# Gelu steps beside the gates, reordered against the head merge

## Chip, cores and metric

One core of a Trainium2 chip runs the whole kernel. The metric is the device time of one execution in microseconds (us); lower is better. Three executions of the kernel before are given.

## The reference, cut to what matters

The program is one decoder block for 1,024 tokens of width 1,024 in float32. Only one place of it concerns the change: the joining of two mixers that run side by side.

```python
y = s5_ssm(u, ...)                                    # (1024 tokens, 768 channels)
z = jax.nn.gelu(y) @ w_glu + b_glu
b_ssm = z[..., :1024] * jax.nn.sigmoid(z[..., 1024:])
wts = jax.nn.softmax(jnp.stack(lses, axis=0), axis=0)  # over the 3 dilated head groups
att = jnp.einsum('gbsh,gbshd->bshd', wts, jnp.stack(outs, axis=0))
b_att = att.reshape(bsz, s, 256) @ w_att_up
mixed = jax.nn.sigmoid(g_ssm) * b_ssm + jax.nn.sigmoid(g_att) * b_att
h = layer_norm(ALPHA * h + (mixed @ w_mix_out + b_mix_out), ln1_g, ln1_b)
```

The gates `g_ssm` and `g_att` are products of the normed input with 2,048 columns of `w_in`. The gelu is the one with the tanh in it.

## The kernel before, in words

Every float32 operand of a product is kept as a high part and a low part, and `mm3` (L99 to L102) multiplies high by high, high by low and low by high. So each tensor that feeds TensorE (PE) has two tiles, and each high/low pair costs one cast on ScalarE (ACT) and one subtraction on VectorE (DVE).

The order of instructions is written by hand: the scheduler is switched to manual, and each engine runs its own instructions in the order in which the program issues them. Side work is woven into the products by generators. `slot()` (L272) first moves the weight stream on (`W.pump`: at most one new load on SP's queue, and one split, an ACT cast `whi` at L136 and a DVE subtraction `wlo` at L137), then runs deferred work, and then lets each generator in `sides` go on to its next `yield`. In the gates a `point()` (L1159) calls `slot()` after every 12 products: once in the middle of a half gate (24 products, `gate_half`) and once at its end. At the end of a half gate, ahead of that second point, the gate's own evacuation is issued: a tanh on ACT (L593), a scale on GpSimd (POOL, L594) and a store to `g_dr` on SP's queue (L595). Splits fall at the point that ends a gate's second half.

`merge_side` (L1043) is the generator that runs beside gates 8 to 15. It does two jobs. For each of 8 token tiles `t` it merges the three head groups: `load` (L1052) brings tile `am` in, `m_main` (L1069) computes softmax weights (three small DVE operations, an exp on ACT at L1076, five small DVE operations), multiplies the heads by them (L1083, DVE) and adds the three groups (L1084 and L1085, POOL); `m_tail` (L1062) transposes the result on PE (L1065) and splits it into `ath` and `atl` (ACT L255, DVE L256). And for each of 12 pieces `i` of the SSM output it computes the gelu: `y_a` loads `yb`; `y_b` squares it on ACT into `yv` (L1099) and does a scale and a product on POOL (L1100, L1101); `y_c` does the tanh on ACT (L1107), a fused add and product on DVE (L1108), the high part `yh` on ACT (L1111) and the low part `yl` on DVE (L1112).

The tile `yv` has one buffer, so the square of a piece can't start until the low part of the piece before has been read from it; pieces 9 to 11 use the buffers of `am` instead:

```python
v = mg_p.tile([128, 4, 128], FT, name="yv", tag="yv", bufs=1)
```

Before the change the order was, per tile: at the first point `m_main(t)` and the load of the next `am`; at the second point `m_tail(t-1)`, then `y_tick(t)`: `y_c` of piece `t-1`, `y_b` of piece `t`, and `y_a` of piece `t+1`. So between `y_b` and `y_c` of one piece stands the next tile's `m_main`. After tile 7 come five more points (`y_tick` for 8 to 12), in which `y_b(i)` goes ahead of `y_c(i-1)`. When gates and merge are through, the gated merge starts (L1179): its first products read `yh` and `yl` of all 12 pieces.

Of the kernel before, what the change touches and what calls it, by code (L numbers as in the profile page):

```python
# [21 lines left out]
NT = SEQ // 128  # L22
# [36 lines left out]
def block_kernel(ctx, tc, I, out, dbg=None):  # L59
# [6 lines left out]
    def open_pool(name, side, **kw):  # L66
        p = tc.tile_pool(name=name, bufs=1, side=side, **kw)
        return p, p.__enter__()
# [27 lines left out]
    def axbank(shape):  # L96
        return ps.tile(list(shape), FT, name="ax", tag="ax", bufs=4)
# [3 lines left out]
        pe.matmul(o, lhsT=lh, rhs=rl, start=False, stop=False)  # L101
        pe.matmul(o, lhsT=ll, rhs=rh, start=False, stop=last)  # L102

# [1 line left out]
    class Stream:  # L105
        def __init__(self):
            self.req = []
# [98 lines left out]
        for i in range(4):  # L206
            W.add(I["wff2"][4 * hc + i], 1024)

# [1 line left out]
    stp = con  # L210

    def ln_rstd(sts, e, extra=None):
# [41 lines left out]
    def split_ps(hi, lo, p):  # L254
        act.copy(hi, p)  # L255
        dve.tensor_sub(lo, p, hi.bitcast(FT))  # L256
# [24 lines left out]
                if next(g, "end") == "end":  # L281
                    sides.remove(g)

# [1 line left out]
    kv_c, kvp = open_pool("kv", "left")  # L285
    mem_c, memp = open_pool("memp", "left")
    st_c, stl = open_pool("start", "right")
# [53 lines left out]
        transpose_in(x, hh, hl, t)  # L341
        act.dma_start(h_dr[t], x)

# [1 line left out]
    T = {}  # L345

    def load_bq(g):
# [331 lines left out]
    for n, (b, part) in enumerate(ustep):  # L679
# [4 lines left out]
        if n in (2, 4):  # L684
            q = 1 + n // 2
# [26 lines left out]
    load_bq(1)  # L712
    par_c, parp = open_pool("par", "right")
    sides.append(params(parp))
# [1 line left out]
    ssm_d = None  # L716

    def start_ssm():
# [164 lines left out]
            ds[b].clear()  # L883
            yield

# [1 line left out]
    att_c, att = open_pool("att", "right")  # L887

    def tok(g, n):
# [147 lines left out]

    sides.insert(0, att_tail())

# [1 line left out]
    state = {"att": att_c, "ssm": ssm_c}  # L1041

    def merge_side():  # L1043
        yf_c, yf = open_pool("yf", "left")
        state["yf"] = yf_c
        ath = yf.tile([128, 2, SEQ], FR, name="ath")
        atl = yf.tile([128, 2, SEQ], FR, name="atl")
        yh = yf.tile([128, 6, SEQ], FR, name="yh")
        yl = yf.tile([128, 6, SEQ], FR, name="yl")
        state.update(ath=ath, atl=atl, yh=yh, yl=yl)  # L1050

        def load(t):  # L1052
            a = mg_p.tile([128, 3, 264], FT, name="am", tag="am", bufs=3)
            sp.dma_start(a, at_dr[:, 128 * t:128 * t + 128, :].rearrange("g p f -> p g f"))
            return a

        mg_c, mg_p = open_pool("mg", "right")
        state["mg"] = mg_c
        nxt = load(0)
        que = deque()  # L1060

        def m_tail(t, a):  # L1062
            p = axbank((128, 2, 128))
            for k in range(2):
                pe.transpose(p[:, k, :], a[:, 0, 128 * k:128 * k + 128], ident)  # L1065
            s = slice(128 * t, 128 * t + 128)
            split_ps(ath[:, :, s], atl[:, :, s], p)

        def m_main(t, a):  # L1069
            w = mg_p.tile([128, 32], FT, name="mw", tag="mw", bufs=2)  # L1070
            M, dd, e, den = w[:, 0:4], w[:, 4:16].rearrange("p (g h) -> p g h", g=3), \
                w[:, 16:28].rearrange("p (g h) -> p g h", g=3), w[:, 28:32]
            dve.tensor_max(M, a[:, 0, 260:264], a[:, 1, 260:264])
            dve.tensor_max(M, M, a[:, 2, 260:264])
            dve.tensor_sub(dd, a[:, :, 260:264], M[:, None, :].to_broadcast([128, 3, 4]))
            act.activation(e, dd, AF.Exp, scale=ATT_SCALE)  # L1076
            dve.tensor_mul(dd, e, a[:, :, 256:260])
            dve.tensor_add(den, dd[:, 0, :], dd[:, 1, :])
            dve.tensor_add(den, den, dd[:, 2, :])
            dve.reciprocal(den, den)  # L1080
            dve.tensor_mul(e, e, den[:, None, :].to_broadcast([128, 3, 4]))
            num = a[:, :, 0:256].rearrange("p g (h d) -> p g h d", h=4)
            dve.tensor_mul(num, num, e.rearrange("p g (h o) -> p g h o", o=1).to_broadcast([128, 3, 4, 64]))  # L1083
            pool.tensor_add(a[:, 0, 0:256], a[:, 0, 0:256], a[:, 1, 0:256])  # L1084
            pool.tensor_add(a[:, 0, 0:256], a[:, 0, 0:256], a[:, 2, 0:256])  # L1085

        def y_a(i):
            b, jh = divmod(i, 2)
            y = mg_p.tile([128, 4, 128], FT, name="yb", tag="yb", bufs=2)
            sp.dma_start(y, y_dr[128 * b:128 * b + 128, 4 * jh:4 * jh + 4, :])  # L1090
            return y

        def y_b(i, y):
            if i <= NT:
                v = mg_p.tile([128, 4, 128], FT, name="yv", tag="yv", bufs=1)
            else:
                v = mg_p.tile([128, 3, 264], FT, name="am", tag="am", bufs=3)
                v = v.rearrange("p g f -> p (g f)")[:, 0:512].rearrange("p (j c) -> p j c", j=4)
            act.activation(v, y, AF.Square)  # L1099
            pool.tensor_scalar(v, v, 0.044715, 1.0, op0=OP.mult, op1=OP.add)  # L1100
            pool.tensor_mul(v, v, y)  # L1101
            return v

        def y_c(i, y, v):
            b, jh = divmod(i, 2)
            js = slice(4 * jh, 4 * jh + 4)
            act.activation(v, v, AF.Tanh, scale=float(np.sqrt(2.0 / np.pi)))  # L1107
            dve.scalar_tensor_tensor(v, v, 1.0, y, op0=OP.add, op1=OP.mult)  # L1108
            vp = v.rearrange("p j c -> p c j")
            yhb, ylb = (q[:, b, :].rearrange("p (c j) -> p c j", j=8)[:, :, js] for q in (yh, yl))  # L1110
            act.activation(yhb, vp, AF.Copy, scale=0.5)  # L1111
            dve.scalar_tensor_tensor(ylb, vp, 0.5, yhb.bitcast(FT), op0=OP.mult, op1=OP.subtract)  # L1112

        ys = {0: y_a(0)}
        vs = {}

        def y_tick(i):
            if i in ys and i > NT:
                vs[i] = y_b(i, ys[i])
            if i - 1 in vs:  # L1120
                y_c(i - 1, ys.pop(i - 1), vs.pop(i - 1))
            if i in ys and i <= NT:
                vs[i] = y_b(i, ys[i])
            if i + 1 < 12:
                ys[i + 1] = y_a(i + 1)

        yield
        for t in range(NT):
            m_main(t, nxt)
            que.append((t, nxt))  # L1130
            if t < NT - 1:
                nxt = load(t + 1)
            yield
            if t:
                m_tail(*que.popleft())
            y_tick(t)
            yield
        for i in range(NT, 13):
            y_tick(i)
            yield  # L1140
            if i == NT:
                m_tail(*que.popleft())

    merged = [False]

    def launch_merge():
        if merged[0] or sides:
            return
        close_pool(state["att"])
        close_pool(state["ssm"])  # L1150
        close_pool(stb_c)
        close_pool(tab_c)
        g = merge_side()
        sides.append(g)
        merged[0] = True
# [16 lines left out]
    close_pool(state["mg"])  # L1172
    ath, atl, yh, yl = (state[k] for k in ("ath", "atl", "yh", "yl"))

# [1 line left out]
    mx_c, mx = open_pool("mx", "right")  # L1176
    xh = actp.tile([128, KB, SEQ], FR, name="acth", tag="acth")
    xl = actp.tile([128, KB, SEQ], FR, name="actl", tag="actl")
# [41 lines left out]
    close_pool(mx_c)  # L1220
    close_pool(state["yf"])

# [1 line left out]
    nat_c, nat = open_pool("nat", "left")  # L1224
    hn = nat.tile([128, NT, D], FT, name="hn")

# [52 lines left out]

    nat_gemm(xh, xl, evac_mix)  # L1280

# [1 line left out]
    ptp_c, ptp = open_pool("ptp", "right")  # L1283
    ph = ptp.tile([128, 4, SEQ], FR, name="ph")
    pl = ptp.tile([128, 4, SEQ], FR, name="pl")
# [44 lines left out]

    nat_gemm(Cat(ph, xh), Cat(pl, xl), evac_xo)

# [1 line left out]
    fh, fl = ph, pl  # L1334
    for t in range(NT):
        defer(t, lambda t=t: dve.scalar_tensor_tensor(hn[:, t, :], hn[:, t, :], ALPHA, bf2, op0=OP.mult, op1=OP.add))
# [157 lines left out]
```

## Time and profile before

| | us |
|---|---|
| three executions | 1945.46, 1943.19, 1945.0 |
| median | 1945.0 |
| span of the profiled execution, first to last instruction | 1943.7 |
| TensorE busy, share of the span | 1885.0 (97%) |
| VectorE busy | 966.7 (50%) |
| ScalarE busy | 563.7 (29%) |
| GpSimd busy | 609.0 (31%) |
| mean granted TensorE clock, 1 being full | 0.990 |

The profile gives the span of the profiled execution but no time of its own for it; the median of the three timed executions is 1.3 us above that span. The head merge and the gelu run from about 700 to 791 us of the span.

### The profile page before, as it was taken

What the parts mean: (1) busy time and instruction counts of PE and PEld (TensorE: products, weight loads), DVE (VectorE), ACT (ScalarE), POOL (GpSimd) and SP (SyncE); (2) the same over time, 40 slices, a digit from 0 to 9 for tenths busy, and PEclk for the clock granted to TensorE, in tenths of its full rate; (3) what the DMA queues carried; (4) which work ended last, traced back from release to release, by engine and by line L of the source; (5) the groups of instructions that cost most, each with busy time, mean ns of one, the idle gap of its engine ahead of it and who ended that gap; (6) DMA issues with size and microseconds to landing.
All of it is one profiled execution on the core that took longest, in us unless ns stands there. A gap on an engine that the chain in (4) does not pass through costs nothing.

```text
span 1943.7 us, 24170 instructions
## 1 busy us (share of the span) xinstructions
PE 1885.0 (97%) x9400; PEld 1619.6 (83%) x9400; DVE 966.7 (50%) x1678; ACT 563.7 (29%) x998; POOL 609.0 (31%) x782
## 2 busy tenths in 40 slices
PE   7899999999999998999999999999999999999996
PEld 7798788889999976788888888788888888888885
DVE  6526846675666666444556445542323223232328
ACT  4324343433332434322124322412121212213121
POOL 3305687474565335322034004401010100101016
PEclk9999999999999999999999999999999999999998
DMA  6545562130120243333511121111111111011102
GB/s 243 184 122 187 183 198 73 34 99 23 55 67 29 75 136 109 118 117 109 185 44 44 44 76 44 44 65 44 55 54 44 44 44 66 32 55 48 62 21 87
DMA packets 82563, 163.26 MB, mean 84 GB/s; under 512 B 19857, under 2 KB 39441, under 8 KB 82449
## 3 DMA queue, kind: packets, MB, share of 16 engines
q1 hardware_dynamic: 75968, 147.30, 22.8%
q10 hardware_dynamic: 5904, 12.85, 1.7%
q0 software_dynamic: 576, 1.57, 0.3%
q8 instruction: 74, 1.21, 0.3%
q14 instruction: 41, 0.33, 0.1%
HBM read 126.99 MB, written 34.70 MB: 83 GB/s over the span
## 4 chain that ended last, share of the span: by engine, by line
PE 86%; DVE 7%; ACT 2%; issue 2%; POOL 2%; DMA 1%; DVEq 0%; SPq 0%; ACTq 0%; POOLq 0%
PE mm L100 26%; PE mm L102 26%; PE mm L101 26%; PE ax L262 1%; DVE wlo L137 1%; PE ax L996 1%; PE ax L969 1%; PE ax L987 1%; PE ax L822 1%; ACT yh L1111 1%; PE ax L845 1%; PE ax L954 1%; PE ax L809 1%; DVE lnst L237 0%; PE ax L846 0%
## 5 line engine op out<-in xcount | busy, mean ns | idle before, releaser
L100 PE MATMUL mm<-acth,whi 128*128 128x512 f32 (+1 forms) x896 | 348.0, 388 | 4.9 <-ACT abst L611 4.6
L102 PE MATMUL mm<-acth,wlo 128*128 128x512 f32 (+1 forms) x896 | 345.5, 386 | 2.5 <-DVE wlo L137 2.5
L101 PE MATMUL mm<-actl,whi 128*128 128x512 f32 (+1 forms) x896 | 345.4, 386 | 0.3 <-DVE actl L256 0.3
L136 ACT CAST whi<-wraw 128x1024 fp32r<-128x1024 f32 (+1 forms) x169 | 168.4, 996 | 419.5 <-PE mm L102 300.9
L137 DVE TENSOR_TENSOR wlo<-wraw,whi 128x1024 fp32r<-128x1024 f32 (+1 forms) x169 | 213.2, 1263 | 146.9 <-ACT whi L136 144.6
L100 PE MATMUL mm<-whi,acth 128*128 128x512 f32 (+1 forms) x704 | 281.7, 400 | 0.0
L102 PE MATMUL mm<-whi,actl 128*128 128x512 f32 (+1 forms) x704 | 270.7, 384 | 0.0
L101 PE MATMUL mm<-wlo,acth 128*128 128x512 f32 (+1 forms) x704 | 270.4, 384 | 0.0
L1350 POOL TENSOR_TENSOR sg<-sg 128x512 f32<-128x512 f32 x64 | 67.8, 1059 | 574.4 <-ACT sg L1349 574.4
L100 PE MATMUL mm<-whi,ph 128*128 128x512 f32 x576 | 224.3, 389 | 0.0
L102 PE MATMUL mm<-whi,pl 128*128 128x512 f32 x576 | 224.1, 389 | 0.0
L101 PE MATMUL mm<-wlo,ph 128*128 128x512 f32 x576 | 224.1, 389 | 0.0
L100 PEld LDWEIGHTS mm<-acth,whi 128*128 128x128 f32 x896 | 171.1, 191 | 38.4 <-ACT abst L611 5.5
L102 PEld LDWEIGHTS mm<-acth,wlo 128*128 128x128 f32 x896 | 170.6, 190 | 36.4 <-DVE wlo L137 3.0
L101 PEld LDWEIGHTS mm<-actl,whi 128*128 128x128 f32 x896 | 171.1, 191 | 32.6 <-DVE actl L256 0.5
L102 PEld LDWEIGHTS mm<-whi,actl 128*128 128x128 f32 x704 | 168.0, 239 | 15.3
L101 PEld LDWEIGHTS mm<-wlo,acth 128*128 128x128 f32 x704 | 168.6, 239 | 14.2
L100 PEld LDWEIGHTS mm<-whi,acth 128*128 128x128 f32 x704 | 167.5, 238 | 15.4
L1352 DVE TENSOR_TENSOR pl<-sg,ph 128x512 fp32r<-128x512 f32 x64 | 44.3, 692 | 261.8 <-ACT ph L1351 261.8
L1368 DVE TENSOR_TENSOR hn<-hn,mm 128x512 f32<-128x512 f32 x128 | 87.0, 685 | 163.7 <-PE mm L102 163.7
L102 PEld LDWEIGHTS mm<-whi,pl 128*128 128x128 f32 x576 | 108.1, 188 | 22.4
L101 PEld LDWEIGHTS mm<-wlo,ph 128*128 128x128 f32 x576 | 108.1, 188 | 22.4
(322 smaller groups left out, 2882.6 us busy)
## 6 DMA issues: line engine op xcount, KB each, us to landing
wraw<-in_wff_dram SPq DMA_DIRECT2D x64, 512.0 KB
wraw<-in_wg_dram SPq DMA_DIRECT2D x16, 512.0 KB
gl<-g_dr SPq DMA_DIRECT2D x32, 256.0 KB
wraw<-in_wqk_dram SPq DMA_DIRECT2D x12, 512.0 KB
wraw<-in_wglu_dram SPq DMA_DIRECT2D x16, 384.0 KB
g_dr<-abst SPq DMA_DIRECT2D x16, 256.0 KB
a_dr<-abst ACTq DMA_DIRECT2D x16, 256.0 KB
b_dr<-abst ACTq DMA_DIRECT2D x16, 256.0 KB
```

The source lines that it names most:

```text
L100: pe.matmul(o, lhsT=lh, rhs=rh, start=first, stop=False)
L101: pe.matmul(o, lhsT=lh, rhs=rl, start=False, stop=False)
L102: pe.matmul(o, lhsT=ll, rhs=rh, start=False, stop=last)
L136: act.copy(h[:, :n], r[:, :n])
L137: dve.tensor_sub(l[:, :n], r[:, :n], h[:, :n].bitcast(FT))
L262: pe.transpose(p[:, k, :], x[:, (4 * b + k) * 128:(4 * b + k + 1) * 128], ident)
L809: pe.matmul(p[:, g, :], lhsT=xe[:, g].rearrange("p j o -> p (j o)"), rhs=d["cm"][:, g, 0:8, :].rearrange("p j o -> p (j o)"), start=True, ...
L822: pe.matmul(p[:, g, :], lhsT=d["bt"][:, g, :], rhs=d["U"][:, g, :], start=True, stop=True)
L845: pe.matmul(p[:, g, :], lhsT=dts[:, g, :], rhs=d["U"][:, g, :], start=True, stop=False)
L1350: pool.tensor_mul(r, r, r)
L1352: dve.tensor_sub(fl[:, i, s], r, fh[:, i, s].bitcast(FT))
L1368: dve.tensor_add(hn[:, t, cs], hn[:, t, cs], p)
```

## The change

The subtraction that makes `yl` leaves `y_c` and becomes a step `y_d` of its own. A new `y_first(i)` does `y_d` of the piece before, then `y_a` of the next piece, then `y_b` of piece `i`. In the loop over tiles `y_first(t)` is issued right behind `m_main(t)` at the first point (ahead of the load of the next `am`), and `y_c(t)` at the second point behind `m_tail(t-1)`. So `y_b` and `y_c` of a piece now stand in one tile, with nothing of `m_main` between them, and `yl` of piece `t-1` stands behind `m_main(t)`. After tile 7, each point does `y_c(i)` and then `y_first(i + 1)`, and the last `yl` has a point to itself, behind that point's weight split. The number of points is as before. Otherwise only comment lines of the source fall away, which moves line numbers.

```diff
@@ -1109,37 +1109,44 @@
             act.activation(yhb, vp, AF.Copy, scale=0.5)
+            lows.append((ylb, vp, yhb))
+
+        def y_d():
+            if not lows:
+                return
+            ylb, vp, yhb = lows.pop()
             dve.scalar_tensor_tensor(ylb, vp, 0.5, yhb.bitcast(FT), op0=OP.mult, op1=OP.subtract)
 
+        lows = []
         ys = {0: y_a(0)}
-        vs = {}
-
-        def y_tick(i):
-            if i in ys and i > NT:
-                vs[i] = y_b(i, ys[i])
-            if i - 1 in vs:
-                y_c(i - 1, ys.pop(i - 1), vs.pop(i - 1))
-            if i in ys and i <= NT:
-                vs[i] = y_b(i, ys[i])
+
+        def y_first(i):
+            y_d()
             if i + 1 < 12:
                 ys[i + 1] = y_a(i + 1)
+            return y_b(i, ys[i])
 
         yield
         for t in range(NT):
             m_main(t, nxt)
             que.append((t, nxt))
+            v = y_first(t)
             if t < NT - 1:
                 nxt = load(t + 1)
             yield
             if t:
                 m_tail(*que.popleft())
-            y_tick(t)
+            y_c(t, ys.pop(t), v)
             yield
-        for i in range(NT, 13):
-            y_tick(i)
+        v = y_first(NT)
+        yield
+        m_tail(*que.popleft())
+        for i in range(NT, 12):
+            y_c(i, ys.pop(i), v)
+            if i < 11:
+                v = y_first(i + 1)
             yield
-            if i == NT:
-                m_tail(*que.popleft())
+        y_d()
```

## Rows read from the trace of the kernel before

**Rows 1.** The page's first part: busy time of each engine, whole span.

```profile
PE 1885.0 (97%) x9400; PEld 1619.6 (83%) x9400; DVE 966.7 (50%) x1678; ACT 563.7 (29%) x998; POOL 609.0 (31%) x782
```

**Rows 2.** Busy time by stretch: window, length, PE, PEld, DVE, ACT, POOL, clock, DMA, GB/s.

```profile
712.82:761.44 48.62, 39.15 (x161) 30.45 (x160) 37.76 (x76) 21.68 (x39) 26.98 (x30) 0.93 0.43 139
...
791.00:830.00 39.00, 39.00 (x172) 32.31 (x173) 16.68 (x23) 10.31 (x18) 10.70 (x11) 1.00 0.42 132
```

**Rows 3.** Waits of PE between 690 and 800 us: total, times, longest.

```profile
PE ax L1065 <- POOL am L1085: 9.9, 6, 2.5
```

**Rows 4.** Timeline of one tile: start, duration, engine, line, operands, [idle before <- releaser].

```profile
742.80 1.30 POOL L1101 TENSOR_TENSOR yv<-yv,yb 128x512 f32<-128x512 f32 x1
742.96 1.15 DVE L1079 TENSOR_TENSOR mw<-mw 128x4 f32<-128x4 f32 x1
...
745.72 0.72 POOL L1084 TENSOR_TENSOR am<-am 128x256 f32<-128x256 f32 x1 [1.63 <-PE mm L102]
745.84 1.15 DVE L1108 SCALAR_TENSOR_TENSOR yv<-yv,yb 128x512 f32<-128x512 f32 x1
...
747.03 1.11 ACT L1111 ACTIVATE yh<-yv 128x512 fp32r<-128x512 f32 x1 [2.27 <-DVE yv L1108]
...
747.64 0.44 PE L1065 MATMUL ax<-cst,am 128*128 128x128 f32 x2 [2.01 <-POOL am L1085]
748.17 1.08 DVE L1112 SCALAR_TENSOR_TENSOR yl<-yv,yh 128x512 fp32r<-128x512 f32 x1 [1.17 <-ACT yh L1111]
```

**Rows 5.** Timeline: the product of the heads (L1083) of tiles 1 and 7.

```profile
711.86 0.96 DVE L1083 TENSOR_TENSOR am<-am,mw 128x768 f32<-128x768 f32 x1
...
760.48 0.96 DVE L1083 TENSOR_TENSOR am<-am,mw 128x768 f32<-128x768 f32 x1
```

**Rows 6.** Timeline 764 to 772: gelu of piece 7, no head merge beside it.

```profile
765.14 0.63 ACT L1099 ACTIVATE yv<-yb 128x512 f32<-128x512 f32 x1 [1.15 <-DVE yl L1112]
765.86 0.62 POOL L1100 TENSOR_SCALAR yv<-yv 128x512 f32<-128x512 f32 x1 [1.83 <-ACT yv L1099]
766.56 1.29 POOL L1101 TENSOR_TENSOR yv<-yv,yb 128x512 f32<-128x512 f32 x1
...
768.55 0.69 DVE L1108 SCALAR_TENSOR_TENSOR yv<-yv,yb 128x512 f32<-128x512 f32 x1 [3.44 <-ACT yv L1107]
769.27 1.14 ACT L1111 ACTIVATE yh<-yv 128x512 fp32r<-128x512 f32 x1 [0.76 <-DVE yv L1108]
770.44 1.09 DVE L1112 SCALAR_TENSOR_TENSOR yl<-yv,yh 128x512 fp32r<-128x512 f32 x1 [1.20 <-ACT yh L1111]
```

**Rows 7.** Timeline: merge of tile 0, no gelu beside it: exp to product of heads.

```profile
704.37 0.21 ACT L1076 ACTIVATE mw<-mw 128x12 f32<-128x12 f32 x1 [5.16 <-DVE mw L1075]
...
705.62 0.96 DVE L1083 TENSOR_TENSOR am<-am,mw 128x768 f32<-128x768 f32 x1
```

**Rows 8.** Timeline: a low part on DVE and a gate's scale on POOL at once.

```profile
782.40 1.08 DVE L1112 SCALAR_TENSOR_TENSOR yl<-am,yh 128x512 fp32r<-128x512 f32 x1 [1.21 <-ACT yh L1111]
783.03 0.88 POOL L594 TENSOR_SCALAR sg<-sg 128x512 f32<-128x512 f32 x1 [0.68 <-ACT sg L593]
```

**Rows 9.** Timeline: a weight split's subtraction on DVE.

```profile
736.98 0.95 DVE L137 TENSOR_TENSOR wlo<-wraw,whi 128x768 fp32r<-128x768 f32 x1
```

**Rows 10.** Timeline: the end of the gelu and the gated merge's first waits.

```profile
788.67 1.09 ACT L1111 ACTIVATE yh<-am 128x512 fp32r<-128x512 f32 x1 [1.12 <-DVE am L1108]
...
789.80 1.07 DVE L1112 SCALAR_TENSOR_TENSOR yl<-am,yh 128x512 fp32r<-128x512 f32 x1 [1.16 <-ACT yh L1111]
790.24 0.82 ACT L136 CAST whi<-wraw 128x768 fp32r<-128x768 f32 x1
...
790.92 0.50 PE L101 MATMUL mm<-yl,whi 128*128 128x512 f32 x1 [0.60 <-DVE yl L1112]
```

**Rows 11.** Timeline of PE: transposes of two neighbouring tiles.

```profile
731.21 0.44 PE L1065 MATMUL ax<-cst,am 128*128 128x128 f32 x2 [1.99 <-POOL am L1085]
...
739.71 0.44 PE L1065 MATMUL ax<-cst,am 128*128 128x128 f32 x2 [0.95 <-POOL am L1085]
```

## The prediction, made before the change was run

> **What bounds the kernel now.** The page's first part says PE: busy 97% of the span, DVE only half of it [rows 1]. That is an average, so the next view is busy time by stretch. While the head merge runs, PE is busy 39.15 of 48.62 us at a mean clock of 0.93; right after it, all of 39.00 us at 1.00 [rows 2]. So in this stage something else sets the pace, and what the stage loses is not made good later: behind it PE is full. PE's waits name the culprit: the merge's transposes (L1065) wait for POOL's sum of the head groups (L1085), 9.9 us in 6 waits [rows 3]. Those sums come at the pace of the loop over tiles on DVE, ACT and POOL: from the product of the heads (L1083) of tile 1 to that of tile 7 are 760.48 - 711.86 = 48.62 us, 8.10 per tile [rows 5], against PE's 5.48 for 24 products (from 739.71 + 0.44 to 747.64 - 2.01) and 0.44 for the transposes, 5.92 in all [rows 4, 11].
>
> The loop now: low part of piece t-1, `m_main(t)` on DVE, L1108 of piece t, its high part on ACT, its low part. DVE stands idle 1.17 for the high part [rows 4]. The rest of the gelu, square to tanh, runs on ACT and POOL beside `m_main`, at a price: a 4-element L1079 takes 1.15 us, ending when POOL's L1101 ends at 744.10, where tile 0 went through the exp and all five small operations in 1.25 (704.37 to 705.62) [rows 7], and L1108 takes 1.15 beside L1084 against 0.69 alone [rows 4, 6]. DVE and POOL keep each other out.
>
> **The change, part by part.** Nothing is computed more or less; instructions move.
>
> *Removed.* Per tile, DVE's wait of 1.17 for the high part, and the two stalls, 1.0 and 0.46: about 2.6 us.
>
> *What the new order waits for.* Square to tanh of piece t loses its cover, because `m_main(t)` now stands ahead of it and the square can't start before the low part of piece t-1, now behind `m_main(t)`, has left the single `yv`. And ACT runs the exp of `m_main(t+1)` behind the high part of piece t, so DVE's wait for ACT doesn't go away: it moves from L1112 to L1077, three small operations further on. All steps lie in one ring: low part, square, L1100, L1101, tanh, L1108, high part, exp, L1083, low part.
>
> *Its length.* Piece 7 of the old kernel ran just this ring without the merge. The square starts at 765.14, 0.03 behind the low part before it; L1108 ends at 769.24, the high part at 770.41, the low part at 771.53: 6.42 us a turn [rows 6]. The merge puts in exp to the end of L1083, 2.21 us in tile 0, where no gelu disturbed it (704.37 to 706.58) [rows 7]; with about 0.1 of overlap at either end, 2.0. POOL's two sums now stand ahead of L1100. They can begin as L1083 ends, but the low part is on DVE by then. Where a low part and a POOL operation meet, POOL's takes 0.88 and ends 0.43 behind the low part (783.91 against 783.48) [rows 8], where such a scale takes 0.62 alone [rows 6]. So I let L1084 end 0.59 behind the low part and L1085 take 0.73, near L1084's 0.72 [rows 4]; L1100 then starts 1.49 behind the low part instead of 0.75, which adds 0.74. If POOL weren't held there, the sums would be over before the square and add nothing: that is the lower end. I take the held case, as rows 8 show this very instruction. Together 6.42 + 2.0 + 0.7 = **9.1 us per tile** against 8.10; lower end 8.4.
>
> *Weight splits* (L137) fall into the second point of every other tile. The 0.95 us [rows 9] used to lie between DVE's steps; now they come when POOL does L1101, and one of the two waits: some 0.6 for the two splits of 768 columns, 0.1 for a small one, 1.3 in all; at the least nothing.
>
> *Start.* Before, no gelu step lay between the L1083 of tiles 0 and 1; now one turn of the ring does. Tile 0 has no low part (1.08 less) but a large split (0.95 or more), so I count a full 9.1. L1083 of tile 7 then ends at 706.58 + 7 x 9.1 + 1.3 = 771.6, against 761.44: 10.2 us late.
>
> *End.* From there the old kernel needed 29.4 us to the last low part (790.87) [rows 10], which PE waits for. New: low part of 6, 1.0; on to L1108 of 7, 4.1 + 0.7; high and low part, 2.3; piece 8 to its L1108, 4.1 and 0.4 for a split; its high part, 1.2. That is 13.8. Pieces 9 to 11 are squared only behind the high part of the piece before (formerly ahead of it): 765.14 to 770.41 is 5.27 [rows 6], with 0.25 for L1100 held by the low part, 5.5 each: 30.3. The last low part has moved past the next point's weight split: the cast ends 1.3 behind the last high part (791.06 against 789.76) [rows 10], then `wlo` 0.95 and the low part 1.08: 33.7, or 4.3 us later than before. POOL's scale for a gate may get between those two on DVE: 0.4 more.
>
> *What costs nothing.* `y_a` passes the load of `am` on SP's queue, an issue of some 0.4 us; both tiles are wanted a full turn later. The gate's tanh (ACT) and scale (POOL) now stand behind the square and L1101, so PSUM banks and the two `sg` buffers come free later; PE's waits list none for them and PE itself waits longer at the transposes. Without that cover the late tanh would cost PE up to the 0.63 of the square per half gate, one of three banks in use, so I count zero.
>
> *Sum.* 10.2 + 4.3 + 0.4 = 14.9 us on the profiled span of 1943.7, whose tail is full PE work and hides none of it. The median of the runs is 1945.0, 1.3 above the span; I add the sum to the median: **1960 us**.
>
> *PE's clock.* Behind a wait of 1.99 the next 24 products took 7.11 us (731.65 to 738.76) instead of 5.48, so part of them ran at 1.2 GHz instead of 2.4, 1.63 us lost [rows 11]. In the merge a turn of 9.1 covers that. The Trainium skill, TensorE: Matmul & The Clock Gate, Part 1, says that the throttled state is the default and that activity releases it. By that rule the longer waits, 9.1 - 5.92 = 3.2, speak against the change: a throttle behind every wait. No run here shows it yet. By the rows, the end is the only bare place: PE has done its gates and the first 15 products some 2.6 us ahead of the last high part, then waits some 3 us more for the low part, and a throttle there adds up to 1.6: 1961.6.
>
> **The rivals.**
> *POOL isn't held by the low part, and splits fall into gaps.* The ring is 8.4: 706.58 + 58.8 = 765.4, 4.0 late; the end shorter by 0.7 + 3 x 0.25 + 0.4, so about 2.5 late: +6.5 to +8, 1952. For it: POOL's starts in the trace are often early. Against it: rows 8.
> *Bare throttle at the end*, +16.5, 1961.6; if slow products filled whole half gates (10.96 + 0.44 per turn, 2.3 more than 9.1), seven turns would add 16 to that, near 1977; rows 11 show recovery within the half, so I give this next to nothing.
> *Faster: PE takes the pace.* If a square didn't have to wait for the low part (were `yv` free in time), `m_main` and high part would overlap with the next square, DVE's own work per tile (2.21 + 1.08 + 0.69 and, by my estimate from the lengths of their like, 1.0 for three small operations and the transposes' low part: 5.0 us) would fit under PE's 5.92, and seven turns from 706.58 would end L1083 of tile 7 at 748.0, 13.4 early, less 4.7 at the end: 1936. The place is the wait of L1099 for L1112, which the trace shows ("<-DVE yl L1112") [rows 6]. It decides where a turn is under (761.44 - 4.7 - 1.3 - 706.58) / 7 = 7.0 us, and the ring of durations alone gives 8.4.
> *No change.* A turn of 6.4 to 7.5 us would give it; nothing in the rows is that short. Also the change could do nothing if the low part were held by ACT in either order, but `yv` then still puts the square later.
>
> **How the numbers follow.** Main case 1960: 0.70. Low case 1952: 0.15. Bare throttle 1961.6 or more: 0.08. Faster: 0.03. No change: 0.04. About 0.2%, 3.9 us, is what a measurement can tell from no change. Faster 0.03, same 0.04, slower 0.93. The range goes from the low case, 1952, to the throttle with all splits at their upper price (two more at 0.6, and 1.5 for the start), 1965.
>
> **What would show it.** Right: L1083 ends some 9 us apart; DVE's L1112 no longer waits for ACT but L1077 does, by 0.5 us or more; L1079 back to 0.16; L1084 stretched beyond 1 us beside L1112; DVE idle ahead of L1108, waiting for the tanh; PE's waits at L1065 near 3 us each; the last low part behind `wlo`. Wrong: L1083 less than 7.5 us apart, squares that start without waiting for L1112, or PE waiting for a bank instead of L1085.

## The result, and the profile of the changed kernel

The changed kernel takes **1962.99 us** (median of 4 runs, 1959.36 to 1963.58), the kernel before 1944.75 on the same chip (4 runs): a ratio of 1.0086, 95% interval 1.0074 to 1.0098. It is slower by 18.2 us; the forecast was 1960.0, with a range from 1952 to 1965. The profiled execution took 1963.19, 1.8 above its span of 1961.4 us; the span before was 1943.7. So 17.7 us have to be found in the trace. Of all executions behind the numbers below one took 8133.02 us (the low part alone late, in the kernel before); it is left out, and its cause is not known.

The page's first part is the average that hides the matter. It answers to [rows 1]:

```profile
PE 1892.8 (97%) x9400; PEld 1624.8 (83%) x9400; DVE 954.4 (49%) x1678; ACT 563.5 (29%) x998; POOL 609.8 (31%) x782
```

PE ran the same 9400 products, for 7.8 us more, and its share is again 97%. DVE did the same 1678 instructions in 12.3 us less: the stalls that the change removes are indeed gone. Added up over the eight tiles, the small operations L1073 to L1081 took 10.7 us less and L1108, over all twelve pieces, 2.4 less, together some 1.6 a tile; a little of it came back in other operations. The time went elsewhere. The waits of PE between 690 and 815 us, as total, times and longest, answer to [rows 3]:

```profile
PE ax L1065 <- POOL am L1085: 17.9, 8, 3.2
PE mm L101 <- DVE yl L1118: 3.1, 1, 3.1
PE mm L100 <- ACT yh L1111: 0.7, 1, 0.7
```

The transposes wait 17.9 us where they waited 9.9, and a wait of 3.1 for the last low part (now L1118) has appeared. Next come the starts of L1083 for the first and last tile, from the timeline, as in [rows 5]:

```profile
705.41 0.96 DVE L1083 TENSOR_TENSOR am<-am,mw 128x768 f32<-128x768 f32 x1
...
770.91 0.96 DVE L1083 TENSOR_TENSOR am<-am,mw 128x768 f32<-128x768 f32 x1
```

Seven turns in 65.50 us: 9.36 us a turn. The product of tile 7 ends at 771.87 where it ended at 761.44. Busy time by stretch, from the second tile's product to the last one's and over the end of the gelu (length, PE, PEld, DVE, ACT, POOL, clock, DMA, GB/s), answers to [rows 2]:

```profile
714.85:770.91 56.06, 41.70 (x157) 32.01 (x156) 28.03 (x75) 21.76 (x39) 29.07 (x30) 0.88 0.37 118
800.00:805.00 5.00, 1.93 (x8) 1.04 (x6) 2.26 (x3) 3.23 (x5) 1.41 (x2) 1.00 0.14 52
805.00:810.00 5.00, 4.27 (x10) 3.40 (x11) 1.32 (x2) 1.67 (x3) 1.24 (x2) 0.50 0.80 236
810.00:815.00 5.00, 5.00 (x19) 4.02 (x19) 0.13 (x1) 1.41 (x2) 0.62 (x1) 0.82 0.69 239
815.00:820.00 5.00, 5.00 (x23) 4.13 (x22) 1.57 (x2) 0.00 (x0) 1.28 (x1) 1.00 0.10 26
```

In the merge PE is busy 41.70 of 56.06 us, and the clock's mean fell from 0.93 to 0.88. DVE is busy for half of the stretch, against 37.76 of 48.62 before. No engine is full there: the pace is that of a ring of waits. Read the turn of tile 2 in the timeline, from L1108 of piece 1 to L1108 of piece 2; it is one of the longer ones, 9.75 us, with a weight split in it (start, duration, engine, line, operands, [idle before <- releaser]; products and some operations left out; the first line is PE's wait in the turn before):

```profile
718.14 0.44 PE L1065 MATMUL ax<-cst,am 128*128 128x128 f32 x2 [3.11 <-POOL am L1085]
...
720.87 0.69 DVE L1108 SCALAR_TENSOR_TENSOR yv<-yv,yb 128x512 f32<-128x512 f32 x1 [2.12 <-ACT yv L1107]
...
721.59 1.14 ACT L1111 ACTIVATE yh<-yv 128x512 fp32r<-128x512 f32 x1 [0.76 <-DVE yv L1108]
...
722.87 0.17 DVE L1077 TENSOR_TENSOR mw<-mw,am 128x12 f32<-128x12 f32 x1 [0.84 <-ACT mw L1076]
...
723.27 0.16 DVE L1079 TENSOR_TENSOR mw<-mw 128x4 f32<-128x4 f32 x1
...
723.89 0.96 DVE L1083 TENSOR_TENSOR am<-am,mw 128x768 f32<-128x768 f32 x1
724.77 1.03 DVE L1118 SCALAR_TENSOR_TENSOR yl<-yv,yh 128x512 fp32r<-128x512 f32 x1
724.93 1.40 POOL L1084 TENSOR_TENSOR am<-am 128x256 f32<-128x256 f32 x1 [4.18 <-DVE am L1083]
725.88 0.63 ACT L1099 ACTIVATE yv<-yb 128x512 f32<-128x512 f32 x1 [3.04 <-issue]
...
726.41 0.72 POOL L1085 TENSOR_TENSOR am<-am 128x256 f32<-128x256 f32 x1
...
727.19 0.69 PE L1065 MATMUL ax<-cst,am 128*128 128x128 f32 x2 [3.13 <-POOL am L1085]
727.22 0.62 POOL L1100 TENSOR_SCALAR yv<-yv 128x512 f32<-128x512 f32 x1
...
727.84 0.96 DVE L137 TENSOR_TENSOR wlo<-wraw,whi 128x768 fp32r<-128x768 f32 x1 [2.04 <-ACT whi L136]
...
727.92 2.01 POOL L1101 TENSOR_TENSOR yv<-yv,yb 128x512 f32<-128x512 f32 x1
...
729.96 0.63 ACT L1107 ACTIVATE yv<-yv 128x512 f32<-128x512 f32 x1 [1.89 <-POOL yv L1101]
...
730.62 0.69 DVE L1108 SCALAR_TENSOR_TENSOR yv<-yv,yb 128x512 f32<-128x512 f32 x1 [1.50 <-ACT yv L1107]
```

Each step of the ring starts about as the one that it needs ends. DVE's small L1079 takes 0.16 again instead of 1.15, the low part no longer waits for ACT, and yet the turn is longer. From 726.41 to 729.93 POOL runs its second sum, the scale and the product one behind the other (the product slowed to 2.01 by a weight split on DVE), and only then come tanh, L1108, high part and exp. Last, the end of the gelu:

```profile
801.02 1.09 ACT L1111 ACTIVATE yh<-am 128x512 fp32r<-128x512 f32 x1 [0.76 <-DVE am L1108]
...
803.43 0.96 DVE L137 TENSOR_TENSOR wlo<-wraw,whi 128x768 fp32r<-128x768 f32 x1 [2.45 <-ACT whi L136]
...
804.31 1.37 DVE L1118 SCALAR_TENSOR_TENSOR yl<-am,yh 128x512 fp32r<-128x512 f32 x1
...
805.73 0.79 PE L101 MATMUL mm<-yl,whi 128*128 128x512 f32 x1 [3.08 <-DVE yl L1118]
```

The low part's input is ready at 802.11; DVE idles 2.45 us, waiting for ACT's cast of the next weight, then does that weight's split, and only then the low part, which PE needs. It ends at 805.68, where it ended at 790.87: 14.8 us late. Behind the wait PE runs at 1.2 GHz (clock 0.50), and is back at 2.4 GHz in all of a window only from 815. Losing half of the 4.27 busy us and 0.18 of the next five gives 2.1 + 0.9 = 3.0 us. The spans say nearly the same: from the product at 805.73 to the end are 1155.7 us, from the same product before (790.92) 1152.8, which is 2.9 less. So 14.8 + 2.9 accounts for the 17.7 of the span: 10.4 in the tile loop, 4.4 at the end, 2.9 of slow clock.

### The profile page after: what moved, and what is told of

It is laid out like the page before. It is cut to its first block, busy times and chain, and to the rows that moved or that the text cites. A ratio compares the mean times of both kernels' runs of the same rounds, so it can differ in the third digit from the quotient of the medians.

```text
span 1961.4 us, 24168 instructions
## 1 busy us (share of the span) xinstructions
PE 1892.8 (97%) x9400; PEld 1624.8 (83%) x9400; DVE 954.4 (49%) x1678; ACT 563.5 (29%) x998; POOL 609.8 (31%) x782
## 3 DMA queue, kind: packets, MB, share of 16 engines
q8 instruction: 74, 1.21, 0.3%
## 4 chain that ended last, share of the span: by engine, by line
PE 56%; DVE 2%; issue 1%; POOL 1%; ACT 0%; DVEq 0%; POOLq 0%; ACTq 0%
PE mm L101 18%; PE mm L102 18%; PE mm L100 18%; PE ax L262 1%; POOL hn L252 0%; DVE lnst L237 0%; DVE wlo L137 0%; DVE rs L224 0%; DVE hn L1375 0%; DVE rs L223 0%; POOL am L1100 0%; POOL am L1101 0%; DVE hn L1381 0%; POOL sg L594 0%; DVE hn L241 0%
## 5 line engine op out<-in xcount | busy, mean ns | idle before, releaser
L100 PEld LDWEIGHTS mm<-whi,ph 128*128 128x128 f32 x576 | 108.1, 188 | 22.4
```

Source lines behind the costliest of these rows:

```text
L100: pe.matmul(o, lhsT=lh, rhs=rh, start=first, stop=False)
```

## The experiments

Two things stand together in the change: square to tanh of a piece moved behind the next merge, and the low part moved behind it. Seven kernels start from the changed one and undo or mend a part of it; four start from the one before. Ratios are to the kernel before, on the same chip. "Turn" is a seventh of the time from the product of the heads of tile 0 to that of tile 7: 7.84 before, 9.36 after.

**Two scratch buffers in the changed kernel.** The rival says that the single `yv` makes the ring. The second buffer lies over constants that are no longer read.

```diff
-    cst = con.tile([128, 516], FT, name="cst")
+    cst = con.tile([128, 660], FT, name="cst")
-    dcol = con.tile([128, G], FT, name="dcol")
+    dcol = cst[:, 516:564]
...
-                v = mg_p.tile([128, 4, 128], FT, name="yv", tag="yv", bufs=1)
+                v = mg_p.tile([128, 4, 128], FT, name="yv", tag="yv", bufs=1) if i % 2 == 0 else \
+                    cst[:, 128:640].rearrange("p (j c) -> p j c", j=4)
```

> Edit: the changed kernel with a second buffer for the gelu's scratch tile, laid over constants that are dead by then, so that the square no longer waits for the low part. My theory: nothing to gain, because the ring also runs through GpSimd's order. GpSimd must add the three head groups of tile t before it may scale the square of piece t, and those adds wait for the product of the heads and then for the low part's hold on the shared access. The turn stays at 9.0 us, the time within 2 us of 1963, though the square itself starts some 3 us earlier. Rival (my prediction put it so): the single buffer is what holds the ring. Then a turn falls by the 0.7 to 1.1 us between the low part and the scale, 1955 to 1958.

Measured: 1961.03 us, 1.0089 [1.0072, 1.0106], turn 9.32. The square now starts early, and nothing comes of it. Timeline of one turn:

```profile
738.70 0.61 ACT L1100 ACTIVATE yv<-yb 128x512 f32<-128x512 f32 x1
...
739.91 0.96 DVE L1083 TENSOR_TENSOR am<-am,mw 128x768 f32<-128x768 f32 x1
...
741.01 1.35 POOL L1084 TENSOR_TENSOR am<-am 128x256 f32<-128x256 f32 x1 [4.29 <-PE mm L102]
...
742.44 1.32 POOL L1085 TENSOR_TENSOR am<-am 128x256 f32<-128x256 f32 x1
...
743.84 0.62 POOL L1101 TENSOR_SCALAR yv<-yv 128x512 f32<-128x512 f32 x1
```

The square is over at 739.31, POOL's scale of it starts at 743.84: POOL idles for 4.29 us and then does the two sums first, because they stand first in its program. By the order of the program both the buffer and POOL's order hold the ring; this run shows that freeing the buffer alone gives nothing. POOL's order changed alone, with one buffer, was not run.

**The low part back in its old place** (for all pieces but the last; the rest as changed).

```diff
-            lows.append((ylb, vp, yhb))
+            if i < 11:
+                dve.scalar_tensor_tensor(ylb, vp, 0.5, yhb.bitcast(FT), op0=OP.mult, op1=OP.subtract)
+            else:
+                lows.append((ylb, vp, yhb))
```

> Edit: the changed kernel with the low part back at the end of the gelu's step for pieces 0 to 10 (the last one stays behind the split). So only the other half of the change is left: square and tanh in one tile, without the merge between them. My theory: the loss comes from the reordering, and the late low part by itself helps. A turn grows from 9.0 to about 10.0 us (DVE waits 1.2 us for the high part and does the low part, 1.1, before it begins the merge, instead of having the first three small operations and the exp's wait there), seven turns, so 1968 to 1971. Rival: the late low part is the harm; then the time goes back towards the kernel before, 1945 to 1953.

Measured: 1969.77, 1.0126 [1.0111, 1.0141], turn 10.49. As expected: within the new order the late low part is a help, of 0.004 in the ratio, some 7 us (1969.77 against 1962.99). What does the harm is the other half, the gelu's first part behind the merge.

**The merge's first part, up to the exp, issued ahead of the gelu's second part**, so that the exp doesn't queue behind the high part on ACT.

```diff
-        def m_main(t, a):
+        def m_main(t, a, part=None, w=None):
...
+            if t < NT - 1:
+                mw = m_main(t + 1, nxt, 0)
             y_c(t, ys.pop(t), v)
```

> Edit: the changed kernel with the first part of the next tile's merge (three small DVE operations and the exp on ScalarE) issued ahead of the gelu's tanh instead of behind its high part. My theory: the exp behind the high part is a link of the ring worth the 0.8 us wait plus the three small operations, so that a turn falls by 1.3 us to about 7.7 and seven turns by 9 us; a bit less, as the three operations now compete with GpSimd's product: 1953 to 1956. Rival: the ring is held by GpSimd and the buffer alone; then the exp was hidden anyway and the time stays within 2 us of 1963.

Measured: 1955.68, 1.0059 [1.0044, 1.0074], turn 8.62 against an expected 7.7, though the time is as expected. The turn is the miss, and that the time agrees is in part luck: seven turns give back 5.2 of the 7.3 us, a shorter slow stretch behind the last low part some 1 by the clock, and the rest is not traced. The timeline has the reason for the turn:

```profile
732.06 1.30 POOL L1105 TENSOR_TENSOR yv<-yv,yb 128x512 f32<-128x512 f32 x1
...
732.22 1.17 DVE L1077 TENSOR_TENSOR mw<-am,mw 128x12 f32<-128x12 f32 x1
```

The small operation on 12 elements now falls beside POOL's product and ends with it (733.39 against 733.36), so the exp starts 1.0 us later than the ring of durations says.

**The old order for the last pieces**: the next square ahead of the second part, the low part at once, for pieces 9 to 11.

```diff
-            y_c(i, ys.pop(i), v)
             if i < 11:
-                v = y_first(i + 1)
+                u = y_b(i + 1, ys[i + 1])
+            y_c(i, ys.pop(i), v)
+            y_d()
+            if i < 10:
+                ys[i + 2] = y_a(i + 2)
+            v = u
```

> Edit: the changed kernel with the kernel before's order for pieces 9 to 11 (square ahead of the tanh of the piece before, each low part at once). The tile loop is untouched. My theory: the last low part comes 6 us earlier (19.3 us behind that of piece 7, as before, instead of 25.8), and PE, which had its 15 products done at 801.4, waits a fraction of a us instead of 0.7 and 3.1; the slow clock behind the 3.1 us wait, 2.9 us, goes too: 4.3 + 2.9 = 7 us, 1955 to 1957. Rival: the slow clock does not hang on that wait but on the waits of the merge before; then only 4 us come back, 1959.

Measured: 1956.33, 1.006 [1.0045, 1.0075]; the last low part ends at 797.91, PE has no wait at the end, and its clock stays at 1.00 there. The span falls by 6.7 us, which is what the changed kernel shows in that place: 3.08 + 0.73 of wait and 2.9 of slow clock. The tile loop (turn 9.35) is untouched, and 11 us of loss remain.

**Only the last low part ahead of the weight split.**

```diff
+            else:
+                y_d()
             yield
-        y_d()
```

> Edit: the changed kernel with only the last piece's low part issued right behind its high part, ahead of the weight split of the next point. My theory: the last low part comes 2.5 us earlier, PE waits some 0.6 instead of 3.1 us for it, and a wait that short is not followed by a stretch of slow clock (0.50 and 0.82 in the two 5 us slices behind it now, 2.9 us of the span): 5 us in all, 1957 to 1959. Rival: the slow stretch belongs to the many waits of the merge before it and stays; then 2.5 us, 1960 to 1961.

Measured: 1957.59, 1.006 [1.0047, 1.0074], turn 9.37. The end's waits and clock:

```profile
PE mm L100 <- ACT yh L1111: 0.7, 1, 0.7
PE mm L101 <- DVE yl L1118: 0.6, 1, 0.6
```

```profile
800.00:805.00 5.00, 3.66 (x15) 2.63 (x15) 2.09 (x2) 3.18 (x5) 1.73 (x2) 1.00 0.28 67
805.00:810.00 5.00, 5.00 (x24) 4.14 (x23) 1.60 (x2) 2.57 (x5) 1.85 (x3) 1.00 0.82 269
```

The same two waits as before the change, 0.7 and 0.6, and no slow stretch behind them. One instruction, placed behind the next weight's split, which itself waits for ACT's cast, was worth 5.4 us by the medians: 2.5 of wait and 2.9 of clock.

**The gelu's first part ahead of POOL's sums.** Two buffers as above, and square, scale and product issued right behind the exp; the low part stays behind the merge. This frees both the buffer and POOL's order.

```diff
             act.activation(e, dd, AF.Exp, scale=ATT_SCALE)
+            v = mid(t)
...
             pool.tensor_add(a[:, 0, 0:256], a[:, 0, 0:256], a[:, 2, 0:256])
+            y_d()
+            return v
...
-            m_main(t, nxt)
+            v = m_main(t, nxt, y_next)
-            v = y_first(t)
```

> Edit: the kernel with two scratch buffers, and in it the gelu's square, scale and product of piece t issued right behind the merge's exp, so that GpSimd does them ahead of the adds of the head groups; the low part stays behind the merge. My theory (GpSimd's order, not the buffer, was the last hold): square to tanh now runs beside the merge and the low part again. By hand a turn is 6.7 to 7.2 us instead of 9.3, seven turns 15 to 18 us: 1944 to 1948, about the kernel before, although its end is still the slow one. Rival (the hold is the exchange of the shared access between VectorE and GpSimd, whatever the order): the turn stays above 8.5 and the time above 1957.

Measured: 1944.21, 0.9993 [0.9984, 1.0002], turn 7.49: the loss is gone, 16.8 us less than with two buffers alone. The square was early in both, so that is what POOL's order is worth once the buffer is free: 12.8 us in the seven turns, most of the rest at the end, where PE's wait fell from 3.1 to 0.8 and no slow stretch follows. The mean turn is a little longer than the 6.7 to 7.2 expected: the four turns without a weight split are 7.02 to 7.22, the three with one 7.66 to 8.19. PE's waits and one turn:

```profile
PE ax L1065 <- POOL am L1086: 11.3, 7, 2.0
PE mm L101 <- DVE yl L1122: 0.8, 1, 0.8
```

```profile
725.54 1.30 POOL L1105 TENSOR_TENSOR cst<-cst,yb 128x512 f32<-128x512 f32 x1
725.58 2.08 DVE L1084 TENSOR_TENSOR am<-am,mw 128x768 f32<-128x768 f32 x1
```

POOL's product starts 0.04 us ahead of DVE's and DVE's takes 2.08 instead of 0.96. In five of the eight tiles the stall that the change removed from a 4-element operation has come back on the largest one; those turns are no longer than the others, 7.12 where there is no split.

**That kernel with the old order for the last pieces** (both edits above together).

> Edit: the kernel with two scratch buffers and the gelu's GpSimd work ahead of the adds, and in addition the old order for pieces 9 to 11. If both readings hold, their gains add up: 1945 or so less the 7 us of the tail, 1936 to 1942, faster than either kernel. Rival: with turns under 7.5 us the products of TensorE take the pace (5.9 us a turn, and 4 half gates behind the last transposes), and the tail's gain shrinks to 2 us or less: 1942 to 1946.

Measured: 1943.71, 0.9993 [0.9984, 1.0002]. The two gains don't add, as the rival said: only 0.8 us of wait was left at the end, and the 0.5 us between the medians is less than a measurement can tell.

**Two buffers in the kernel before** (the first edit, nothing else).

> Edit: the kernel before with two scratch buffers and nothing else, a control. The square no longer waits for the low part (1.1 us earlier), so GpSimd's product is over earlier and holds the merge's small operations up for less: by hand a turn of 7.3 to 7.6 instead of 8.1, 3 to 5 us in all, 1940 to 1942. Rival: the kernel before is held by VectorE's order alone (it waits for the high part and does everything in between); then nothing moves, 1944 to 1946.

Measured: 1943.24, 0.9988 [0.9979, 0.9997], turn 7.77 against 7.84. The time lies between the theory's 1940 to 1942 and the rival's 1944 to 1946; the turn of 7.3 to 7.6 missed. In the old order the buffer was not the hold: POOL's product starts earlier, and now it is the small L1075 that ends with it, in place of L1079.

```profile
722.45 1.29 POOL L1102 TENSOR_TENSOR yv<-yv,yb 128x512 f32<-128x512 f32 x1
722.60 1.16 DVE L1075 TENSOR_TENSOR mw<-am,mw 128x12 f32<-128x12 f32 x1
```

L1075 stands ahead of the exp, so the exp comes later by as much. Most of the 1.9 us fits another place: the two waits at the end, 0.7 and 0.6, are gone from the list.

**Only the late low part, in the kernel before** (with two buffers, without which the square would wait for it).

```diff
+            lows.append((ylb, vp, yhb))
...
             m_main(t, nxt)
+            y_d()
```

> Edit: the kernel before with two scratch buffers and only the low part moved behind the next tile's merge; the gelu's order is that of before, so the merge still stands between the product on GpSimd and the tanh. My theory: the late low part alone does no harm: it takes VectorE's wait for the high part (1.2 us) away, but the exp stands behind high part and square on ScalarE, 0.6 us more of waiting than in the changed kernel; by hand a turn of 7.4 us, 1939 to 1943, within 3 us of the control. Rival (the late low part is what makes the changed kernel slow): 1950 or more.

Measured: 1944.29 (the median of nine), 0.9998 [0.9988, 1.0007], turn 7.59. A little above the expected 1939 to 1943; but the question is answered: the late low part, one of the two halves of the change, is harmless by itself. The turn is shorter by a quarter of a microsecond, and the whole gives nothing that can be told from no change.

**Scale and product as one step on DVE, in the kernel before.** (y^2 + 1/0.044715) y, with the constant moved into the tanh's scale: the same value up to rounding. POOL then does only the sums and the gates' scales.

```diff
-            pool.tensor_scalar(v, v, 0.044715, 1.0, op0=OP.mult, op1=OP.add)
-            pool.tensor_mul(v, v, y)
...
+            dve.scalar_tensor_tensor(v, v, 1.0 / 0.044715, y, op0=OP.add, op1=OP.mult)
...
-            act.activation(v, v, AF.Tanh, scale=float(np.sqrt(2.0 / np.pi)))
+            act.activation(v, v, AF.Tanh, scale=float(0.044715 * np.sqrt(2.0 / np.pi)))
```

> Edit: the order and the single scratch buffer of the kernel before, but the gelu's inner factor y(1 + 0.044715 y^2) as one fused VectorE step (square plus 1/0.044715, times y, the constant moved into the tanh's scale) behind the next tile's merge, instead of two GpSimd steps beside it. The computation is the same up to rounding. My theory: the kernel before is paced by VectorE and GpSimd shutting each other out in the merge's small steps. VectorE gets 0.6 us more work and loses 1.4 us of stalls per turn: 7.8 falls to 6.9 or so, 6 us, and each of the last pieces gets 1.2 shorter: 1936 to 1941. Rival: VectorE's own work and its wait for the high part set the turn, stalls or not; then the extra step costs what it saves, 1943 to 1947.

Measured: 1943.91, 0.9993 [0.9985, 1.0002], turn 7.51 against an expected 6.9. The theory missed, the rival held: the stalls of the small operations go, and the added step (0.69) and the wait for the high part, which stays (1.21), take their place.

**That step together with two buffers and the late low part**, with the square issued ahead of the previous tanh.

```diff
+        def y_m(i, y, v):
+            dve.scalar_tensor_tensor(v, v, 1.0 / 0.044715, y, op0=OP.add, op1=OP.mult)
...
             if i in ys:
+                y_m(i, ys[i], vs[i])
+            if i >= NT:
+                y_d()
...
             m_main(t, nxt)
+            y_d()
```

> Edit: as the last, with two scratch buffers, the square issued ahead of the tanh of the piece before, the fused step behind the second VectorE step of the piece before, and the low part behind the next tile's merge. My theory: VectorE waits for the high part no more and its stalls are gone; a turn of 6.0 to 6.5 us, near the 5.9 that PE needs, so that PE loses 0.5 us a tile instead of 2, and no slow clock: 1931 to 1937. Rival: a wait for the exp (behind high part and square on ScalarE) takes the place of the others, 7.3 us a turn as with the late low part alone: 1940 to 1944.

Measured: **1937.99 us** (1937.0 to 1940.3), 0.9962 [0.9949, 0.9976], turn 7.10: faster than both kernels. The time lies between the theory's 1931 to 1937 and the rival's 1940 to 1944: the ring is shorter, but not as short as 6.0 to 6.5. Waits of PE between 690 and 815, and part of the timeline:

```profile
PE ax L1065 <- POOL am L1085: 8.2, 7, 2.3
```

```profile
724.51 0.32 SPq L595 DMA_DIRECT2D g_dr<-sg  x1
...
725.41 0.39 SPq L1090 DMA_DIRECT2D yb<-y_dr  x1
...
729.37 0.63 ACT L1100 ACTIVATE cst<-yb 128x512 f32<-128x512 f32 x1 [3.06 <-DMA yb<-y_dr]
...
731.43 0.68 DVE L1104 SCALAR_TENSOR_TENSOR cst<-cst,yb 128x512 f32<-128x512 f32 x1
...
732.88 0.17 DVE L1077 TENSOR_TENSOR mw<-mw,am 128x12 f32<-128x12 f32 x1 [0.28 <-ACT mw L1076]
...
733.96 0.96 DVE L1083 TENSOR_TENSOR am<-am,mw 128x768 f32<-128x768 f32 x1
...
736.02 0.63 ACT L1100 ACTIVATE yv<-yb 128x512 f32<-128x512 f32 x1 [1.88 <-DVE yl L1120]
```

No wait is left at the end. DVE runs the merge's small operations without a stall, but the square waits. In four of the pieces 1 to 7 it is for the load of its `yb`, 2.73 to 3.61 us. The load for the square at 729.37 was issued at 725.41; L1110 had released its buffer at 724.01, but a gate's store, which waits for POOL's scale, and a weight load stood ahead of it in SP's queue. In the other three it is for the low part that still reads the square's own buffer, 1.76 to 2.28 us. The rows point to that load and that buffer as what sets the pace now; an earlier issue of the load, or a third buffer of either kind, was not tried.

## Why the prediction came out as it did

**The direction and the mechanism were right.** *What the new order waits for* was the ring, and it is there link by link: L1077 waits for ACT (0.84), the low part doesn't, L1079 is back to 0.16, L1084 is stretched to 1.40 beside the low part, DVE idles 1.50 to 2.12 ahead of L1108, and the transposes wait up to 3.2. The last low part stands behind `wlo`. All of these stood in the list of what would show it; only that PE's waits would be near 3 us each holds for four of the eight, since in the others slow products fill part of the turn or, in the first, the ring has only begun.

**Its length and the weight splits.** 9.1 us a turn and 1.3 in all for the splits make 9.3; the trace has 9.36, the first turn 9.44, then four of 9.0 to 9.2 and two of 9.8. L1083 of tile 7 was to end at 771.6 and ends at 771.87. The choice in it, that POOL's L1084 is held by the low part, is borne out by its 1.40 us; the lower end of 8.4 did not come. (In the low case the end comes out 4.7 - 1.85 = 2.85 late, not 2.5, and the terms of the upper end add up to 1964.3, not 1965; neither moves the forecast.)

**The start and the end.** The first turn was counted as a full 9.1 and is 9.44. From the end of that L1083 to the end of the last low part the text has 33.7 and 0.4; the trace has 805.68 - 771.87 = 33.8. The *sum* of 14.9 stands against 14.8. One reading there was off without touching the sum: PE was to have its products done 2.6 us ahead of the last high part, and it waited 0.73 for it; some 1.5 of that are slow products behind the last transposes (25.79 busy us at a mean clock of 0.94 from 771 to 800), and the longer wait behind, for the low part, covers it.

**What was mis-sized is *PE's clock*.** The text named the end as the only bare place, the only one where no later wait covers a slow PE, expected a wait of about 3 us there (it is 3.08), and priced the throttle behind it at up to 1.6 from [rows 11], as a rival at 1961.6 and not in the main sum. It came and cost 2.9: there are 14 slow products behind the wait, the last at 811.45, where the half gate of [rows 11] lost 1.63. That is the whole gap between 1960.0 and 1963. The runs show that the slow stretch hangs on this wait: with the last low part put forward, the waits are 0.7 and 0.6 and the clock is 1.00.

How long it lasts does not follow from the wait. In the kernel with two buffers the same wait of 3.08 us, up to 801.79, is followed by 6 slow products, and the row below gives a loss of about 1.1 us (3.21 busy us at 0.66):

```profile
800.00:805.00 5.00, 3.21 (x8) 2.58 (x9) 2.38 (x3) 1.72 (x4) 2.04 (x3) 0.66 0.79 239
```

Nor does every such wait bring one. In the changed kernel the products behind the wait of 3.11 us at 718.14 ran at full clock, those behind 3.13 us at 727.19 at a mean of 0.66:

```profile
718.58:724.06 5.48, 5.48 (x25) 4.16 (x23) 2.28 (x11) 1.88 (x3) 2.09 (x3) 1.00 0.38 115
727.88:735.98 8.10, 8.10 (x24) 6.01 (x23) 5.14 (x13) 2.30 (x5) 3.80 (x3) 0.66 0.42 133
```

So a price of 1.6 was within what the runs show, 2.9 is what this execution got, and what sets the length stays open. The section cited in the prediction, Part 1 of the Trainium skill's TensorE: Matmul & The Clock Gate, calls the throttled state the default, which activity releases. The rows agree in that the clock falls to its lower level behind waits, 0.50 behind 3.08 us; that it would do so behind every wait is not borne out, by the 1.00 behind 3.11 us. In the merge the fall of the mean clock to 0.88 lies under the ring, as the text said it would: behind each slow stretch PE still waits, for POOL's sums or, after the last transposes, for the last high and low part.

**The rival that ended faster had its condition wrong.** It was to decide by whether `yv` was free in time. The run with two buffers freed it, and the turn stayed at 9.32. The prediction's own working had the second hold in it, since it counted POOL's sums ahead of L1100, but only as a lengthening of 0.7. With POOL's order changed as well the turn is 7.49, and the kernel is level with the one before, still not faster.

**What the change removes was costed about right and did not matter.** The stalls were put at 1.0 and 0.46 a tile; the operations that had them are shorter by 1.6 a tile, a stall of L1077 (0.58 instead of 0.17 in most tiles) among them that the text left out. PE never sees the saving, because the ring passes through DVE, ACT and POOL in series and DVE waits in it anyway.

## What to carry to other kernels

Before a step is put behind other work to hide a wait, write down the ring that its result closes, through the program order of every engine that it passes, the idle ones included: here POOL, busy 31% of the span, held the loop by doing two sums first. Freeing a buffer was worth nothing here while an in-order engine still stood in the same place; each of the two has to be tried alone and together (POOL's order alone was not). And look at the last pass by itself: what is late there is bare, and here a wait of 3.08 us in front of a full PE cost its length and a slow stretch behind it, of 2.9 us in one kernel and 1.1 in another.

## What the hardware showed that was not expected

In each of these pairs the one of POOL and DVE that starts second pays, whatever its size: a 12-element operation took 1.17 us instead of 0.17 beside POOL's product, DVE's 128x768 product 2.08 instead of 0.96 where POOL's had started 0.04 us earlier, and POOL's 128x512 product 2.01 instead of 1.29 beside a weight split. The Trainium skill, SBUF — State Buffer, section Who interferes with whom, has an exclusive lock between the two, where DVE's instruction has two SBUF inputs and POOL's reads SBUF, and the order of issue decides who is kept out; these rows, all of that kind, agree with it. So where two such operations meet, their order chooses the victim. The kernel that gained, by 7 us, took scale and product off POOL and had two buffers and the late low part as well; the runs with only a part of that gave 2 us or less.

The slow clock behind one wait of 3.08 us outlasted the wait: 0.50 in all of the window from 805 to 810, and 0.82 in the one behind it, with PE full. Behind 0.7 and 0.6 us none was seen. Waits of 3.1 us elsewhere were followed by anything from no slow product to 14.
